# The fourth plain chunk of a gated network: its low weights move from VectorE to GpSimd, and last in its first product

## The chip, the cores and the metric

The kernel runs on one core of a Trainium2 chip. A core has five engines with queues of their own: TensorE (PE: matmuls, and transposes that are matmuls against an identity), VectorE (DVE), ScalarE (ACT), GpSimd (POOL) and SyncE (SP), which here issues the DMA loads and stores. Each runs its instructions in program order and waits at semaphores for the others. The metric is the device time of one execution in microseconds (us); less is better.

## The reference, cut to what matters

The program is one inference step of a trunk of two layers. Each layer mixes tokens by attention and then runs a gated network with a convolution of width 3 between its two projections. 512 latent and 128 context tokens, a width of 1024 and an inner width of 2816 give:

```python
def conv_ffn(h, w_up, conv_w, conv_b, w_down):
    u = h @ w_up
    up = jnp.pad(u, ((0, 0), (1, 1), (0, 0)))
    u = up[:, :-2] * conv_w[0] + up[:, 1:-1] * conv_w[1] + up[:, 2:] * conv_w[2] + conv_b
    a, gt = jnp.split(u, 2, axis=-1)
    return (jax.nn.silu(a) * gt) @ w_down

for l in range(DEPTH):            # DEPTH = 2
    ...                           # attention, norms, residuals
    fp = conv_ffn(hp, ffn_w_up[l], ffn_conv_w[l], ffn_conv_b[l], ffn_w_down[l])
    fs = conv_ffn(hs, ffn_w_up[l], ffn_conv_w[l], ffn_conv_b[l], ffn_w_down[l])
    ...
```

The change is in the first product, `h @ w_up`, of both layers.

## The kernel before, in words

**Tiling.** `h` is kept transposed, features on the partitions, tokens in the columns. The 5632 outputs of `w_up` are worked in 22 pairs of a value chunk and a gate chunk of 128 outputs each; `(p, i)` is pair `p`, value (`i` = 0) or gate (`i` = 1). Products are exact to more than one pass: a weight tile `wr`, loaded from memory by SP (`fetch`, L1195), is cast on ACT to a high part `wh` (L1203), and the rest, `wl = wr - wh`, is made by a subtract (L1204) on DVE or on POOL, whichever `split` is given. In the same way the columns have a high and a low part. `block_product` (L1237) multiplies 512 inputs by 322 columns in twelve matmuls: for each of four blocks of 128 inputs `wh` by the high columns, `wl` by the high columns, and `wh` by the low columns. With `lows=True` the four with `wl` come last.

From the third pair on, a scheme with seven products of half-size blocks in place of eight is used; its weights are sums of weight blocks (`block_sums`, L1224 to L1227), and `value`, `corner` and `sum_parts` split them (tiles `vh`, `vl`, `ah`, `al`, `wh`, `wl`). The first two pairs (`PLAIN = 2`) are four *plain* chunks, `chunks[0]` to `chunks[3]`, each with all eight half-size products, since at that time the columns are not complete: tokens are still coming out of the attention's last projection. `plain0` runs the first two products of a chunk ("11" into a `ux` bank, "21" into a `uy` bank), copies the first on ACT (`c`, L1258) and adds it to the second on DVE (L1329); `plain1` runs the others later.

**What stands around the change.** At that point the last token tile (tile 4) is still being finished (`fin0`): on DVE the residual (L400), a scaling (L412) and a shift (L419), with ACT's sums of squares (L370) and three small POOL instructions between (two `v` at L372, `ro` at L379). Its eight transposes on PE (`tr`, L120) run in two groups of four between the chunks. Behind L419 DVE makes the block differences of the columns (L255, L249, with ACT's casts, L248).

The code names the engine of each step, and a scheduler puts each engine's instructions in an order of its own from the code's order, the dependences and its own estimate of times. So an edit in one line also reorders the queues of DVE, ACT, POOL and SP. `bk.get` and `bk.put` hand out PSUM banks: a product or a group of transposes that takes a bank waits until the bank's last reader is done; the second group of four transposes takes the bank that L1329 of the third chunk reads. The four weight tiles `wr` in `wp` go round as well: a load waits for the cast and the subtract that read the tile before it.

The lines to follow are: L1204 (the subtract), L1329 (the add of a plain chunk), L1348 (which engine subtracts for the fourth chunk), L1355 (the loop that runs the third and fourth chunk) and L1195 (loads).

Of the kernel before, what the change touches and what calls it, by code (L numbers as in the profile page):

```python
# [44 lines left out]
TH = 322  # L45
# [59 lines left out]
def hybrid_step(ctx: ExitStack, tc: tile.TileContext, A, O):  # L105
    nc = tc.nc
# [9 lines left out]
    def mm(*a, **k):  # L116
        pe(nc.tensor.matmul(*a, **k))  # L117
# [10 lines left out]
    def pool(name, bufs=1, side="left", **k):  # L128
        return tc.tile_pool(name=name, bufs=bufs, side=side, reuse_waits="tile", **k)
# [356 lines left out]
    def na_v_put(vt, c, src):  # L486
        return nc.scalar.copy(vt[:, c], src.rearrange("p (a d) -> p a d", a=4))
# [18 lines left out]
    with ExitStack() as s:  # L506
# [155 lines left out]
        for c in range(NT):  # L662
            v_part(7, (c,))
            i = na_v_put(vts_of[0], c, vb[c][:, 0:256])
# [490 lines left out]
    def ffn(l, hT, hT_close, xold, xnew, nxt, todo, late, late_close, side, back, first, fin0, after=None):  # L1155
# [28 lines left out]
        with ExitStack() as s2:  # L1184
# [3 lines left out]
            ws, raws, done = first.ws, first.raws, set(first.ws)  # L1188
            nr = [len(raws)]

            def fetch():
                while nr[0] < len(need) and (nr[0] < 4 or need[nr[0] - 4] in done):
                    p, i = need[nr[0]]
                    raw = wp.tile([P, KC, P], F32, tag="wr", name="wr")
                    nc.sync.dma_start(raw, rows(w_up, 0, 8, (p + i * FC) * P, P))  # L1195
                    raws[p, i] = raw
                    nr[0] += 1

            def pair_of(own, tags, n):
                return [own.tile([P, n, P], F32R, tag=x, name=x) for x in tags]  # L1200

            def split(src, hl, low):
                nc.scalar.copy(hl[0], src)  # L1203
                low.tensor_sub(hl[1], src, f32(hl[0]))  # L1204

            def plain(p, i, low):
                ws[p, i] = pair_of(wp, ("wh", "wl"), KC)
                split(raws[p, i], ws[p, i], low)
                done.add((p, i))
                fetch()  # L1210
# [26 lines left out]
            def block_product(u, w, h, b, first, last=True, lows=False):  # L1237

                seq = [(k, n) for k in range(4) for n in range(3)]
                if lows:  # L1240
                    seq.sort(key=lambda kn: kn[1] == 1)
                for i, (k, n) in enumerate(seq):
                    mm(u, w[n == 1][:, 4 * h + k, :], hT.B[b][n == 2][:, k, :], start=first and i == 0,
                       stop=last and i == 11, skip_group_check=True)
# [11 lines left out]
            def copied(name, p, u):  # L1256
                small[name, p] = sw2.tile([P, TH], F32, tag=name, name=name)
                return nc.scalar.copy(small[name, p], u)  # L1258
# [8 lines left out]
            def block(p, i, j):  # L1267
                c0 = 1 + (2 * TH + 1) * i + TH * j
                return sums(p)[:, c0 : c0 + TH]
# [49 lines left out]
                    q, t = outs.popleft()  # L1319
                    nc.sync.dma_start(actd[q], t)  # L1320

            def plain0(p, i):

                x = banks["p", p, i] = bk.get("ux")
                block_product(x[:, 0:TH], ws[p, i], 0, "11", True)
                c = copied("c1", (p, i), x[:, 0:TH])
                y = bk.get("uy")
                block_product(y[:, 0:TH], ws[p, i], 1, "21", True)
                a = nc.vector.tensor_add(block(p, i, 0), y[:, 0:TH], small.pop(("c1", (p, i))))  # L1329
                bk.put(y)  # L1330
                return c, a
# [13 lines left out]
            chunks = [(p, i) for p in range(PLAIN) for i in range(2)]  # L1345
            plain(*chunks[2], nc.vector)
            fin0.last(*zip(*(plain0(*c) for c in chunks[:2])))
            plain(*chunks[3], nc.vector)  # L1348
            swb = s2.enter_context(pool("swb", 1, side))
            hT.begin(swb, ("22", "1"))  # L1350
            late[0]()
            hT.first(0)
            value(PLAIN, nc.vector)
            for c in chunks[2:]:
                plain0(*c)  # L1355
            late[1]()
            hT.first(1)
            u = banks["x", PLAIN][:, 0:TH]
# [119 lines left out]
    def gqa_w(c0, u, own=None):  # L1478
        return wsplit(rows(wqkv, 2 * u, 2, c0, 512), 2, 512, None, own)

    wkv = []
    hT, hp2, late, xmp = ffn(
        0, hT, hp1.close, lambda t: xres[0][t], lambda t: xres[1][t], (1, 1, 0, NS),
        ((0, 5), (1, 1), (1, 0), (1, 2), (1, 4)), late, xmp.close, "right", "left", first, fin,
# [305 lines left out]
    for hq in range(2):  # L1790
        for n, t in enumerate(((4, 0, 1, 2, 3), (0, 1, 2, 3, 4))[hq]):
# [3 lines left out]
            i = 5 * hq + n  # L1795
# [90 lines left out]
    def y_out(t):  # L1886
        return O["y_sample"][0, t * P : (t + 1) * P, :] if t < 4 else O["y_prompt"][0]

    _, _, _, xmp = ffn(
        1, hT, r_h3.close, lambda t: xres[2][t], y_out, None, ((1, 5),), late, xmp.close, "left", "right", first, fin  # L1890
    )
# [70 lines left out]
```

## Time and profile before

| | us |
|---|---|
| median of 3 runs | 1549.0 (1548.19 to 1549.32) |
| the profiled execution | 1550.43 |
| its span in the profile | 1548.6 |
| PE busy | 1513.5 (98% of the span) |
| DVE busy | 1022.3 (66%) |
| ACT busy | 854.0 (55%) |
| POOL busy | 702.2 (45%) |

The clock that PE was granted was 0.998 of full speed over the span. The stretches that the change touches are at about 360 to 400 us (layer 0) and 1100 to 1140 us (layer 1). In a timeline, a row gives the start, the length, the engine, the line and the tiles (out<-in); `x2` groups neighbouring instructions, and a bracket gives the time that the engine idled ahead of it and what ended the idling. Numbers in matmul shapes are partitions by columns.

### The profile page before, as it was taken

The numbers are of one execution on the slowest core, as the hardware profiler recorded it, in microseconds if no ns is written. First come the engines' busy times: TensorE is split into PE (matmuls) and PEld (weight loads), VectorE is DVE, ScalarE is ACT, GpSimd is POOL, SyncE is SP. The second block draws the span as 40 slices with busy tenths as digits, with TensorE's granted clock in tenths as the row PEclk, the third lists the DMA queues.
The fourth block names the chain that finished last, engine by engine and source line by source line (L and its number), as shares of the span: only waits on it lengthen the run. The fifth ranks groups of instructions, "written<-read, shape, count | busy, mean of one in ns | idle before, by whom it ended". The sixth has DMA issues, their size and how long they took to land.

```text
span 1548.6 us, 26098 instructions
## 1 busy us (share of the span) xinstructions
PE 1513.5 (98%) x9709; PEld 1343.4 (87%) x9709; DVE 1022.3 (66%) x1648; ACT 854.0 (55%) x1624; POOL 702.2 (45%) x606
## 2 busy tenths in 40 slices
PE   6999999999999999999999999999999999999998
PEld 5988998888999999978887878778899999988886
DVE  4553343659877666755757877773988887786554
ACT  5664564646655555554544447763665665564443
POOL 1554564432355455525443464532235666542433
PEclk9999999999999999999999999999999999999999
DMA  9745454253565665388574421015433335447664
GB/s 324 199 123 161 121 134 116 64 189 125 176 225 182 222 190 162 111 279 272 174 238 153 131 67 44 2 34 196 153 115 114 120 110 158 132 161 251 226 220 131
DMA packets 196666, 243.99 MB, mean 158 GB/s; under 512 B 11484, under 2 KB 153020, under 8 KB 196540
## 3 DMA queue, kind: packets, MB, share of 16 engines
q1 hardware_dynamic: 186704, 235.74, 47.8%
q10 hardware_dynamic: 9836, 6.59, 2.5%
q8 instruction: 76, 1.25, 0.3%
q14 instruction: 50, 0.41, 0.1%
HBM read 214.38 MB, written 26.34 MB: 155 GB/s over the span
## 4 chain that ended last, share of the span: by engine, by line
PE 63%; DVE 5%; ACT 2%; issue 2%; POOL 2%; DMA 1%; POOLq 0%; DVEq 0%; ACTq 0%
PE ux L117 18%; PE acc L117 17%; PE uz L117 8%; PE gp L117 5%; PE uy L117 4%; PE po L117 3%; PE y L117 2%; PE s L117 2%; PE tp L120 2%; PE ada L117 1%; DMA wr<-in_ffn_w_down 1%; DVE t L1281 1%; POOL wl L180 1%; DMA wr<-in_ffn_w_up 1%; DVE wl L180 1%
## 5 line engine op out<-in xcount | busy, mean ns | idle before, releaser
L180 POOL TENSOR_TENSOR wl<-wr,wh 128x1024 fp32r<-128x1024 f32 x70 | 173.8, 2487 | 239.8 <-ACT wh L178 228.7
L1204 POOL TENSOR_TENSOR wl<-wr,wh 128x1024 fp32r<-128x1024 f32 x76 | 183.6, 2438 | 46.9 <-ACT wh L1203 43.3
L117 PE MATMUL ux<-B,wh 128*128 128x322 f32 x832 | 200.0, 311 | 0.9 <-ACT u L1258 0.9
L1281 DVE SCALAR_TENSOR_TENSOR t<-C,cw,t 128x644 f32<-128x644 f32 x176 | 156.4, 888 | 51.3 <-ACT t L1279 50.7
L178 ACT CAST wh<-wr 128x1024 fp32r<-128x1024 f32 x140 | 145.5, 1048 | 53.8 <-DMA wr<-in_ffn_w_down 41.1
L117 PE MATMUL acc<-wh,alo 128*128 128x512 f32 x440 | 172.3, 392 | 0.3 <-DVE alo L1173 0.3
L117 PE MATMUL acc<-wl,ahi 128*128 128x512 f32 x440 | 171.9, 391 | 0.5 <-POOL wl L180 0.5
L117 PE MATMUL acc<-wh,ahi 128*128 128x512 f32 x440 | 171.9, 391 | 0.0
L117 PE MATMUL uz<-B,wh 128*128 128x322 f32 x640 | 156.2, 312 | 0.9 <-ACT v L1258 0.9
L117 PEld LDWEIGHTS ux<-B,wh 128*128 128x128 f32 x832 | 143.6, 189 | 3.3 <-issue 1.2
L1173 DVE TENSOR_TENSOR alo<-ain,ahi 128x384 fp32r<-128x384 f32 (+1 forms) x88 | 81.8, 948 | 88.9 <-ACT ahi L1171 88.6
L117 PE MATMUL ux<-B,wl 128*128 128x322 f32 x416 | 129.5, 311 | 3.0 <-DVE wl L1204 3.0
L117 PE MATMUL qk<-hT,wh 128*128 128x384 f32 (+1 forms) x512 | 122.3, 315 | 0.0
L117 PEld LDWEIGHTS uz<-B,wh 128*128 128x128 f32 x640 | 110.9, 189 | 4.4 <-ACT v L1258 1.5
L1204 POOL TENSOR_TENSOR vl<-wr,vh 128x1024 fp32r<-128x1024 f32 x38 | 96.4, 2537 | 24.6 <-ACT vh L1203 24.3
L1203 ACT CAST wh<-wr 128x1024 fp32r<-128x1024 f32 x84 | 84.8, 1049 | 40.9 <-DVE wr L1227 40.6
L1279 ACT ACTIVATE t<-C,cw 128x644 f32<-128x644 f32 x88 | 78.6, 893 | 47.8 <-DVE C L1309 40.2
L180 DVE TENSOR_TENSOR wl<-wr,wh 128x1024 fp32r<-128x1024 f32 x70 | 91.4, 1315 | 19.3 <-ACT wh L178 18.7
L117 PE MATMUL uz<-B,wl 128*128 128x322 f32 x320 | 99.6, 311 | 0.3 <-POOL wl L1204 0.3
L117 PEld LDWEIGHTS acc<-wl,ahi 128*128 128x128 f32 x440 | 82.6, 188 | 18.9 <-POOL wl L180 0.9
L117 PEld LDWEIGHTS acc<-wh,alo 128*128 128x128 f32 x440 | 82.5, 188 | 18.7 <-DVE alo L1173 1.1
L117 PEld LDWEIGHTS acc<-wh,ahi 128*128 128x128 f32 x440 | 82.6, 188 | 17.7
(259 smaller groups left out, 3858.2 us busy)
## 6 DMA issues: line engine op xcount, KB each, us to landing
wr<-in_ffn_w_up SPq DMA_DIRECT2D x88, 512.0 KB
wr<-in_ffn_w_down SPq DMA_DIRECT2D x88, 512.0 KB
wr<-in_ada_w SPq DMA_DIRECT2D x72, 512.0 KB
act<-act SPq DMA_DIRECT2D x44, 321.0 KB
wr<-in_na_w_qkv SPq DMA_DIRECT2D x24, 512.0 KB
mod<-modrow SPq DMA_DIRECT2D x20, 512.0 KB
ain<-act SPq DMA_DIRECT2D x44, 192.0 KB
wf<-in_ada_w SPq DMA_DIRECT2D x16, 512.0 KB
```

The source lines that it names most:

```text
L117: pe(nc.tensor.matmul(*a, **k))
L120: pe(nc.tensor.transpose(*a, **k))
L178: i = nc.scalar.copy(hi, raw)
L180: j = (low or nc.vector).tensor_sub(lo, raw, f32(hi))
L1173: pin(nc.vector.tensor_sub(lo[:, 0 : c1 - c0], ain[:, 0 : c1 - c0], f32(hi[:, 0 : c1 - c0])))
L1203: nc.scalar.copy(hl[0], src)
L1204: low.tensor_sub(hl[1], src, f32(hl[0]))
L1279: nc.scalar.activation(t, taps(0), AF.Identity, bias=cw[:, 3, n : n + 1], scale=cw[:, 1, n : n + 1])
L1281: nc.vector.scalar_tensor_tensor(t, taps(d), cw[:, w, n : n + 1], t, op0=ALU.mult, op1=ALU.add)
```

## The change

The fourth plain chunk's low weights are made by GpSimd, and its first product does its four low-weight matmuls last:

```diff
-            def plain0(p, i):
+            def plain0(p, i, lows=False):
 
                 x = banks["p", p, i] = bk.get("ux")
-                block_product(x[:, 0:TH], ws[p, i], 0, "11", True)
+                block_product(x[:, 0:TH], ws[p, i], 0, "11", True, lows=lows)
...
             plain(*chunks[2], nc.vector)
             fin0.last(*zip(*(plain0(*c) for c in chunks[:2])))
-            plain(*chunks[3], nc.vector)
+            plain(*chunks[3], nc.gpsimd)
...
             for c in chunks[2:]:
-                plain0(*c)
+                plain0(*c, lows=c == chunks[3])
```

Both networks run this code, so each engine's order changes at two places of the program. On POOL, layer 0, around the tile finishing before (`v0` and `ro` are the small instructions, `vl_4780` is a subtract of the fourth gated pair):

```order
L372 TENSOR_SCALAR v0_4369<-sso_4367,v0_4053 128x1
L379 TENSOR_TENSOR ro_4372<-v0_4369,mhalf_74 128x1
L372 TENSOR_SCALAR v0_4488<-sso_4486 128x1
L372 TENSOR_SCALAR v0_4494<-sso_4492,v0_4488 128x1
L379 TENSOR_TENSOR ro_4497<-v0_4494,mhalf_74 128x1
L1204 TENSOR_TENSOR vl_4780<-wr_4420,vh_4779 128x1024
```

and now:

```order
L372 TENSOR_SCALAR v0_4369<-sso_4367,v0_4053 128x1
L379 TENSOR_TENSOR ro_4372<-v0_4369,mhalf_74 128x1
L1204 TENSOR_TENSOR wl_4504<-wr_4409,wh_4503 128x1024
L372 TENSOR_SCALAR v0_4488<-sso_4486 128x1
L372 TENSOR_SCALAR v0_4494<-sso_4492,v0_4488 128x1
L379 TENSOR_TENSOR ro_4497<-v0_4494,mhalf_74 128x1
L1204 TENSOR_TENSOR vl_4780<-wr_4420,vh_4779 128x1024
```

The subtract `wl_4504` of the fourth chunk stands directly behind the `ro` that L400 needs and ahead of the two `v0` and the `ro` that L419 needs.

On DVE, layer 0, from L419 of the last token tile to the L1329 of the fourth chunk (`C_4565<-uy_4552` is the third chunk's, `C_4565<-uy_4583` the fourth's), before:

```order
L419 SCALAR_TENSOR_TENSOR xm_4364<-xm_4364,ro_4497,mod_4360 128x512 x2
L1204 TENSOR_TENSOR wl_4504<-wr_4409,wh_4503 128x1024
L255 TENSOR_TENSOR hF_3968<-hF_3968 128x4x190
L249 TENSOR_TENSOR B221_4513<-hF_3968,B220_4512 128x4x190
L1204 TENSOR_TENSOR vl_4534<-wr_4411,vh_4533 128x1024
L249 TENSOR_TENSOR B11_4515<-hF_3968,B10_4514 128x4x190
L1329 TENSOR_TENSOR C_4565<-uy_4552,c1_4550 128x322
L1204 TENSOR_TENSOR al_4705<-wr_4413,ah_4704 128x512
L1329 TENSOR_TENSOR C_4565<-uy_4583,c1_4581 128x322
```

and now:

```order
L419 SCALAR_TENSOR_TENSOR xm_4364<-xm_4364,ro_4497,mod_4360 128x512 x2
L255 TENSOR_TENSOR hF_3968<-hF_3968 128x4x190
L1204 TENSOR_TENSOR vl_4534<-wr_4411,vh_4533 128x1024
L1204 TENSOR_TENSOR al_4705<-wr_4413,ah_4704 128x512
L249 TENSOR_TENSOR B221_4513<-hF_3968,B220_4512 128x4x190
L249 TENSOR_TENSOR B11_4515<-hF_3968,B10_4514 128x4x190
L1329 TENSOR_TENSOR C_4565<-uy_4552,c1_4550 128x322
L1224 TENSOR_TENSOR wr_4413<-wr_4413 128x512
L1204 TENSOR_TENSOR al_4784<-wr_4507,ah_4783 128x512
L1329 TENSOR_TENSOR C_4565<-uy_4583,c1_4581 128x322
```

The subtract of `wl_4504` is gone; `al_4705`, which stood behind the third chunk's L1329, stands ahead of it; one block sum (L1224) and `al_4784`, which came later, stand ahead of the fourth chunk's.

On SP, the loads and stores with their waits (names in the brackets are semaphores of DVE, ACT, POOL and of DMA queues), before:

```order
L406 DMA xres_0_3_96<-xo_4276 128x1024 [waits DMAHW6_49,DMAHW2_49,DVE_49]
L1195 DMA wr_4413<-in_ffn_w_up 128x8x128 [waits DMAHW3_49,DVE_49]
L1195 DMA wr_4420<-in_ffn_w_up 128x8x128 [waits DVE_49,Activation_49]
L406 DMA xres_0_4_97<-xo_4362 128x1024 [waits DMAHW0_49,DVE_49]
L1195 DMA wr_4507<-in_ffn_w_up 128x8x128 [waits DVE_49,Activation_49]
```

and now:

```order
L406 DMA xres_0_3_96<-xo_4276 128x1024 [waits DMAHW6_49,DMAHW2_49,DVE_49]
L1195 DMA wr_4413<-in_ffn_w_up 128x8x128 [waits DMAHW3_49,DVE_49]
L1195 DMA wr_4420<-in_ffn_w_up 128x8x128 [waits Pool_49]
L1195 DMA wr_4507<-in_ffn_w_up 128x8x128 [waits DVE_49]
L406 DMA xres_0_4_97<-xo_4362 128x1024 [waits DMAHW0_49,DVE_49]
```

The load of `wr_4507` stands ahead of a store of the residual and waits for DVE alone, where the load of `wr_4420` ahead of it waits for POOL's new subtract. On ACT the cast `ah_4783` of `wr_4507` moves from behind the fourth chunk's `c` copy to ahead of the third's.

## Rows read from the trace of the kernel before

**Rows 1.** The page: busy times (part 1), one of PE's costliest groups (part 5).

```profile
PE 1513.5 (98%) x9709; PEld 1343.4 (87%) x9709; DVE 1022.3 (66%) x1648; ACT 854.0 (55%) x1624; POOL 702.2 (45%) x606
...
L117 PE MATMUL ux<-B,wh 128*128 128x322 f32 x832 | 200.0, 311 | 0.9 <-ACT u L1258 0.9
```

**Rows 2.** Timeline of PE, layer 0: start us, length us, what, [idle before <-releaser].

```profile
368.41 0.31 PE L117 MATMUL ux<-B,wl 128*128 128x322 f32 x1
...
373.87 0.42 PE L117 MATMUL ux<-B,wl 128*128 128x322 f32 x1 [1.75 <-DVE wl L1204]
...
377.38 1.27 PE L120 MATMUL tr<-ident,xm 128*128 128x128 f32 x8
```

**Rows 3.** Timeline of PE at the same place of layer 1.

```profile
1114.22 0.41 PE L117 MATMUL ux<-B,wl 128*128 128x322 f32 x1 [1.30 <-DVE wl L1204]
```

**Rows 4.** List of waits of PE's weight loads, 372 to 380 us: total, times, longest.

```profile
PEld tr L120 <- DVE C L1329: 0.2, 1, 0.2
```

**Rows 5.** Timeline of DVE, layer 0, 363 to 384 us.

```profile
363.75 1.42 DVE L419 SCALAR_TENSOR_TENSOR xm<-xm,ro,mod 128x512 f32<-128x512 f32 x2 [1.09 <-POOL ro L379]
...
365.70 1.21 DVE L1204 TENSOR_TENSOR wl<-wr,wh 128x1024 fp32r<-128x1024 f32 x1
...
368.56 1.28 DVE L412 TENSOR_TENSOR xm<-xo,mod 128x512 f32<-128x512 f32 x2
...
371.26 1.42 DVE L419 SCALAR_TENSOR_TENSOR xm<-xm,ro,mod 128x512 f32<-128x512 f32 x2 [1.02 <-POOL ro L379]
372.59 1.22 DVE L1204 TENSOR_TENSOR wl<-wr,wh 128x1024 fp32r<-128x1024 f32 x1
373.73 0.94 DVE L255 TENSOR_TENSOR hF<-hF 128x760 f32<-128x760 f32 x1
374.59 0.94 DVE L249 TENSOR_TENSOR B<-hF,B 128x760 fp32r<-128x760 f32 x1
375.45 1.22 DVE L1204 TENSOR_TENSOR vl<-wr,vh 128x1024 fp32r<-128x1024 f32 x1
376.58 0.94 DVE L249 TENSOR_TENSOR B<-hF,B 128x760 fp32r<-128x760 f32 x1
377.45 0.48 DVE L1329 TENSOR_TENSOR C<-uy,c 128x322 f32<-128x322 f32 x1
377.85 0.68 DVE L1204 TENSOR_TENSOR al<-wr,ah 128x512 fp32r<-128x512 f32 x1
...
381.91 1.50 DVE L262 TENSOR_TENSOR hF<-hF 128x1288 f32<-128x1288 f32 x1
...
383.72 3.42 DVE L263 TENSOR_TENSOR hF<-hF 128x1288 f32<-128x1288 f32 x1
```

**Rows 6.** Timeline of POOL, layer 0.

```profile
364.06 0.86 POOL L379 TENSOR_TENSOR ro<-v,mhalf 128x1 f32<-128x1 f32 x1
...
383.38 2.41 POOL L1204 TENSOR_TENSOR vl<-wr,vh 128x1024 fp32r<-128x1024 f32 x1 [12.15 <-ACT vh L1203]
```

**Rows 7.** Timeline of POOL, layer 1.

```profile
1109.66 0.93 POOL L372 TENSOR_SCALAR v<-sso 128x1 f32<-128x1 f32 x1 [4.04 <-ACT junk L370]
```

**Rows 8.** Timeline of DVE, layer 1.

```profile
1109.25 1.28 DVE L412 TENSOR_TENSOR xm<-xo,mod 128x512 f32<-128x512 f32 x2
...
1111.62 1.42 DVE L419 SCALAR_TENSOR_TENSOR xm<-xm,ro,mod 128x512 f32<-128x512 f32 x2 [0.68 <-POOL ro L379]
...
1117.80 0.48 DVE L1329 TENSOR_TENSOR C<-uy,c 128x322 f32<-128x322 f32 x1
```

**Rows 9.** Timeline of SP, layer 0: the load for the fourth gated pair's gate.

```profile
373.89 0.37 SPq L1195 DMA_DIRECT2D wr<-in_ffn_w_up  x1
```

**Rows 10.** Timeline of ACT, layer 0.

```profile
362.91 1.04 ACT L1203 CAST wh<-wr 128x1024 fp32r<-128x1024 f32 x1
...
374.71 0.83 ACT L248 CAST B<-hF 128x760 fp32r<-128x760 f32 x1 [1.13 <-DVE hF L255]
...
377.66 0.62 ACT L1203 CAST ah<-wr 128x512 fp32r<-128x512 f32 x1 [1.44 <-DMA wr<-in_ffn_w_up]
```

## The prediction

> **What bounds the kernel now.** I read the busy times first. The reader is to see TensorE (PE) busy for 1513.5 of 1548.6 us while VectorE (DVE), ScalarE (ACT) and GpSimd (POOL) stand at 66, 55 and 45% [rows 1]. So an edit on another engine counts only where PE waits for that engine, and its price is the change in such a wait. The second view is PE's order of time around the fourth plain chunk. PE waits there 1.75 us in layer 0 and 1.30 us in layer 1 for the low weights that DVE makes at L1204 [rows 2, 3]: 3.05 us in all, the most that taking these waits away alone can give. The third view is the list of waits just behind. The eight transposes that follow the chunk take 1.27 us, and the list says that their weight load waited 0.2 us for L1329, DVE's add of the third chunk (chunks[2]) [rows 2, 4]. That small wait is the important one: it sits 3.5 us behind the big one, and on DVE the two waits' releasers stand in one unbroken row of work. From the L419 at 371.26 to the L1329 that ends at 377.93 each instruction starts as the one before it ends [rows 5]. If PE comes earlier to the transposes, it waits there for the same row of DVE work. So the question is not how soon the low weights are there, but when DVE reaches L1329 of the third chunk.
>
> The fourth view is that row on DVE, with what starts it, and POOL's beside it. L419 waited for POOL's ro (1.02 us, 371.26) [rows 5]; ro follows two small v on POOL, and these follow the residual work L400 and L412 on DVE. In layer 1 one sees how v is tied to DVE: v, one number per partition, took 0.93 us and ended at 1110.59, just after L412 ended at 1110.53; L419 began 1.09 us after that L412 ended [rows 7, 8].
>
> **The change part by part.**
>
> *Low weights last.* The four low-weight products of the fourth chunk's first product go behind its eight others. The number of matmuls stays. Eight matmuls now run ahead of the first that needs the low weights, so POOL may take until well after the time at which PE waited before. Cost nothing.
>
> *Taken from DVE.* One L1204 of 128x1024, a step of 1.14 us (372.59 to 373.73) [rows 5].
>
> *Added to POOL.* The same subtract; POOL's rows for this shape take 2.41 us [rows 6]. It stands directly behind the ro that ended at 364.92 (364.06 + 0.86), ACT's cast of its high weights had ended by 363.95 (362.91 + 1.04) [rows 10], and so it does not wait until the fourth chunk: it starts about when the L419 beside that ro ends, 365.17 (363.75 + 1.42), and ends at 367.58. PE needs it after 372, so for PE it is early by over 4 us.
>
> *What that does to DVE.* At 365.70 DVE wants to start its own L1204, for the third chunk [rows 5]. The trace shows what becomes of a DVE instruction with two SBUF inputs that starts beside a big POOL subtract: L263 took 3.42 us, where L262, of the same shape, took 1.50. POOL's vl had started at 383.38 and ended at 385.79; L263 ended at 387.14, that is 1.35 us after it [rows 5, 6]. I read this as a full stop: DVE's instruction does nearly all of its 1.50 us after POOL's has ended. Applied to the wl at 365.70 (1.21 us alone, 0.14 of it taken off as in L263's case): it ends at 367.58 + 1.07 = 368.65 instead of 366.91, 1.74 us late. Bounds: 0 if there were no such stop, and 1.9 if nothing is taken off. I take 1.74, since L263's row is the same pair of operations.
>
> [...]
>
> *PE at the third chunk.* Its first low-weight matmul ran at 368.41 [rows 2]; it now waits until about 368.7. That is 0.3 us, and it is lost ahead of the wait below, so it does not add to it.
>
> *The row on DVE behind it.* Everything to L412 is moved by the 1.74 us: L412, 368.56 + 1.28 = 369.84 before, ends at 371.58. From there I use layer 1's 1.09 us for v, v, ro: L419 starts at 372.67, 1.41 late (some slack in layer 0 is used up) [rows 5, 8]. Behind it the new order counts. The fourth chunk's wl (1.14) is gone, but an al, which stood behind L1329 of the third chunk, now stands ahead of it (0.68 long; 0.60 as a step, since each step is 0.08 shorter than the row's length). From L419's start to L1329's end: 1.33 + 0.86 + 1.13 + 0.60 + 0.86 + 0.87 + 0.48 = 6.13 us, where it was 6.67 (371.26 to 377.93) [rows 5]. So L1329 ends at 372.67 + 6.13 = 378.80: **0.87 us later** than before.
>
> *What PE makes of it in layer 0.* With the 1.75 gone and 0.3 added PE reaches the transposes at about 375.9 instead of 377.38, does four of the eight and then waits for L1329 until 378.80. The wait of 1.75 is not gained: it has moved to the transposes and grown to over 2.4, and PE goes on 0.87 later.
>
> *Layer 1.* The same instructions stand there with the same durations. L412 (1109.25 + 1.28 = 1110.53) is followed at once by v, v, ro, so there is no slack: L419 goes from 1111.62 to 1113.36, and L1329 ends at 1113.36 + 6.13 = 1119.49 instead of 1118.28: **1.21 us later** [rows 7, 8].
>
> *A copy on ACT and its load.* The ah cast that ran at 377.66 now stands ahead of the third chunk's c copy, and its load ahead of a store. Issue to cast took 3.8 us (373.89 to 377.66) [rows 9, 10]. The load now goes when DVE's wl of the third chunk is done, at about 368.7; with 3.8 us it is there at 372.5 and costs nothing, since L1329 wants c only at 378.3. With twice that, 376.3, it would still let ah, c and two casts on ACT finish near 379, about 0.5 us per layer. I take 0.
>
> *Later on.* At the start of the gate chunks, in layer 1, a t (L1279) now stands ahead of the u copy on ACT for which PE waited 0.9 us in the whole run [rows 1], and DVE's block sums come earlier by the al that has left them. Bounds -0.6 and +0.9; I take +0.3, nearer to the middle.
>
> **Sum:** 0.87 + 1.21 + 0.3 = +2.4 us. The rows are of an execution of 1550.43 us (span 1548.6), 1.4 above the median 1549.0; a few us in so many do not depend on that, so the forecast is 1549.0 + 2.4 = **1551.4 us**.
>
> **The rivals.**
>
> *A, POOL and DVE do not stop each other (ends not slower).* The wl at 365.70 runs as before, L419 starts at 371.26, and L1329 ends at 371.26 + 6.13 = 377.39, 0.54 earlier; in layer 1 as much (1111.62 + 6.13 = 1117.75). PE gains 1.1 us, 1547.9. For it: L419, the neighbour of ro, took its usual 1.42. Against it: L263's 3.42 and v's 0.93. It decides at one place: whether the third chunk's wl on DVE takes about 1.2 or about 2.9 us. [...]
>
> *B, the whole wait of 3.05 us is gained.* That needs the transposes not to wait for L1329: 1546.0. For it: they waited only 0.2 before. Against it: the DVE row is shorter by 0.54 alone, while PE would come 1.75 earlier. It would need DVE's other work to move too.
>
> *C, the load is what is late.* Two weight loads are now issued within about 1 us (367.6 and 368.7). If they share the DMA engines with more than the load of the row, and the ah cast comes at 377 instead of 372.5, then ah (0.62) and c (about 0.4) are done at 378.1, the two casts for B (0.83 each) [rows 10] at 379.7, L249 at 380.6, and L1329 at 381.0: 2.2 us later than forecast in a layer. In one layer 1553.6, in both 1555.8. Against it: 8 us and more from issue to landing would be twice the row's 3.8.
>
> *D, POOL's subtract starts only behind the residual work,* say as L412 ends at 369.84. Then it runs to 372.25 and stops L419 in place of the wl: L419, 1.42 long, goes on from there, a microsecond later than at 371.26, and L1329 ends at 377.39 + 1.0 = 378.4, 0.46 later than before; in both layers 0.9, 1549.9. Against it: nothing in POOL's order keeps the subtract waiting so long.
>
> **How the numbers follow.** Forecast (+1 to +4) 0.55; A 0.12; B 0.05; C 0.15; D 0.13. About 0.2%, 3.1 us, is what a measurement of this kernel can tell from no change. The forecast's own range is 1550 to 1553.5: about a third of its chance is above +3.1 when the end bounds add up (0.5 from the load in each layer, 0.9 at u). Slower: 0.18 + 0.13 of C = 0.31. Faster: of B most, and a little of A where the order later on helps, 0.07. Within 0.2%: 0.62. The range takes in A, D and one layer of C: 1546.8 to 1554.2.
>
> **What would show it.** Right: POOL's wl near 365.2, DVE's wl of the third chunk taking 2.9 us, L419 over a microsecond late, no wait at the fourth chunk's wl, and a wait of over 2 us at the transposes for L1329, in both layers. Wrong: DVE's wl at 1.2 us (A); a wait of PE at the transposes under 0.5 us (B); an ACT wait for wr ahead of c that ends after 376 (C); POOL's wl that starts after 369 (D).

## The result and the profile after

The changed kernel takes 1553.62 us (median of 7 runs, 1552.59 to 1557.54) against 1549.17 for the kernel before (7 runs, 1547.7 to 1549.7): 4.45 us slower, a ratio of 1.0033 with a 95% interval of 1.0024 to 1.0043. That is a loss clear of the noise. The forecast was +2.4 us, with the chance of "within 0.2%" twice that of "slower"; the time lies 0.1 us above the forecast's own range (1550 to 1553.5) and inside the wider one that takes in the rivals. The forecast's 1549.0 was the median of the first three of these seven runs of the kernel before. The profiled execution of the changed kernel took 1552.95 us, its span is 1551.2.

The busy times say as little as before: PE is at 98%, DVE at 66% as in [rows 1].

```profile
PE 1514.3 (98%) x9709; PEld 1345.8 (87%) x9709; DVE 1028.8 (66%) x1646; ACT 853.3 (55%) x1624; POOL 712.0 (46%) x608
```

The timeline of DVE in layer 0 (columns as in [rows 5]) shows the stop and what it moves:

```profile
361.83 1.42 DVE L419 SCALAR_TENSOR_TENSOR xm<-xm,ro,mod 128x512 f32<-128x512 f32 x2 [1.09 <-POOL ro L379]
...
363.78 2.82 DVE L1204 TENSOR_TENSOR wl<-wr,wh 128x1024 fp32r<-128x1024 f32 x1
...
368.25 1.28 DVE L412 TENSOR_TENSOR xm<-xo,mod 128x512 f32<-128x512 f32 x2
...
370.33 1.41 DVE L419 SCALAR_TENSOR_TENSOR xm<-xm,ro,mod 128x512 f32<-128x512 f32 x2 [0.40 <-POOL ro L379]
...
373.66 0.68 DVE L1204 TENSOR_TENSOR al<-wr,ah 128x512 fp32r<-128x512 f32 x1
...
375.98 0.48 DVE L1329 TENSOR_TENSOR C<-uy,c 128x322 f32<-128x322 f32 x1
```

The third chunk's L1204 takes 2.82 us, where [rows 5] has 1.21. On POOL beside it (columns as in [rows 6]):

```profile
362.97 2.54 POOL L1204 TENSOR_TENSOR wl<-wr,wh 128x1024 fp32r<-128x1024 f32 x1
368.56 0.42 POOL L372 TENSOR_SCALAR v<-sso 128x1 f32<-128x1 f32 x1 [3.04 <-ACT junk L370]
```

The new subtract runs from 362.97 to 365.51; DVE's ends at 366.60, 1.09 us after it. Alone it takes 1.21 us [rows 5], so nearly all of its work was done behind POOL's end, as with L263 (1.35 of 1.50). The two profiles differ by 1.93 us ahead of all this: the same matmul, the first of the third chunk, starts at 368.17 before and at 366.24 after. That comes from the first 80 us of the two executions and is taken off below. PE before, at five places (first product of the third chunk, first of the value weights, in layer 0; the same two and the first of `plain1` in layer 1):

```profile
368.17 0.40 PE L117 MATMUL ux<-B,wh 128*128 128x322 f32 x1
...
378.40 0.39 PE L117 MATMUL ux<-B,vh 128*128 128x322 f32 x1
...
1108.99 0.39 PE L117 MATMUL ux<-B,wh 128*128 128x322 f32 x1
...
1118.76 0.40 PE L117 MATMUL ux<-B,vh 128*128 128x322 f32 x1
...
1122.39 0.31 PE L117 MATMUL ux<-B,wh 128*128 128x322 f32 x1
```

and after, with the wait ahead of the second four transposes:

```profile
366.24 0.39 PE L117 MATMUL ux<-B,wh 128*128 128x322 f32 x1
...
376.52 0.66 PE L120 MATMUL tr<-ident,xm 128*128 128x128 f32 x4 [2.20 <-DVE C L1329]
376.93 0.40 PE L117 MATMUL ux<-B,vh 128*128 128x322 f32 x1
...
1107.91 0.39 PE L117 MATMUL ux<-B,wh 128*128 128x322 f32 x1
...
1118.07 0.66 PE L120 MATMUL tr<-ident,xm 128*128 128x128 f32 x4 [2.22 <-DVE C L1329]
1118.48 0.40 PE L117 MATMUL ux<-B,vh 128*128 128x322 f32 x1
...
1123.65 0.31 PE L117 MATMUL ux<-B,wh 128*128 128x322 f32 x1
```

The wait at the low weights [rows 2, 3] is gone and a wait of 2.2 us stands at the transposes in both layers. Differences after minus before, place by place: -1.93, -1.47 in layer 0; -1.08, -0.28 and +1.26 in layer 1; and +2.37 at the program's last matmul. So PE loses 0.46 us at the transposes of layer 0, 0.80 at those of layer 1, **1.54 between two places of layer 1 where no wait stands at all**, and 0.39 and 1.11 us in the long stretches of gate chunks behind. The sum is 4.30 us, and the medians differ by 4.45.

The 1.54 us are the clock. Busy time by windows of 1 us in layer 1 (stretch, its length, then PE, PEld, DVE, ACT and POOL busy with counts, the granted TensorE clock, DMA share and GB/s):

```profile
1118.00:1119.00 1.00, 0.93 (x7) 0.93 (x8) 1.00 (x3) 0.24 (x1) 0.00 (x0) 1.00 0.00 0
1119.00:1120.00 1.00, 1.00 (x8) 1.00 (x7) 1.00 (x3) 0.97 (x2) 0.00 (x0) 0.76 0.00 0
1120.00:1121.00 1.00, 1.00 (x6) 1.00 (x5) 1.00 (x3) 0.15 (x2) 0.00 (x0) 0.50 0.00 0
1121.00:1122.00 1.00, 1.00 (x5) 1.00 (x5) 1.00 (x3) 0.84 (x2) 0.00 (x0) 0.50 0.00 0
1122.00:1123.00 1.00, 1.00 (x5) 1.00 (x5) 1.00 (x3) 0.00 (x0) 0.00 (x0) 0.53 0.02 8
1123.00:1124.00 1.00, 1.00 (x9) 1.00 (x8) 1.00 (x1) 0.15 (x1) 0.00 (x0) 1.00 0.00 0
```

Behind the wait the granted clock stands at 0.50, the lower of its two levels (1.2 in place of 2.4 GHz), for 0.48 + 1.0 + 1.0 + 0.94 = 3.4 us, and each matmul takes about twice its time. Layer 0 had a wait just as long in this execution and no such stretch.

POOL and DVE met once more behind this place, with the roles changed. In layer 1, timelines of DVE and of POOL:

```profile
1124.41 1.49 DVE L263 TENSOR_TENSOR hF<-hF 128x1288 f32<-128x1288 f32 x1
```

```profile
1124.98 9.19 POOL L1204 TENSOR_TENSOR vl<-wr,vh 128x1024 fp32r<-128x1024 f32 x1 [13.14 <-ACT vh L1203]
```

L263, which took 3.42 us beside POOL's vl in the kernel before [rows 5, 6], started 0.57 us ahead of that subtract here. It took its 1.49 us, and POOL's subtract took 9.19 us in place of 2.41: DVE ran six instructions one behind the other until 1131.87, and POOL's ended 2.3 us after that. In layer 0 POOL's started first (381.90 against 382.86), and L263 took 3.31 us.

### The profile page after: what moved, and what is told of

Its sections match the earlier page's. It is cut to its first block, busy times and chain, and to the rows that moved or that the text cites. A ratio compares the mean times of both kernels' runs of the same rounds, so it can differ in the third digit from the quotient of the medians.

```text
span 1551.2 us, 26092 instructions
## 1 busy us (share of the span) xinstructions
PE 1514.3 (98%) x9709; PEld 1345.8 (87%) x9709; DVE 1028.8 (66%) x1646; ACT 853.3 (55%) x1624; POOL 712.0 (46%) x608
## 5 line engine op out<-in xcount | busy, mean ns | idle before, releaser
L1204 POOL TENSOR_TENSOR wl<-wr,wh 128x1024 fp32r<-128x1024 f32 x78 | 188.7, 2440 | 43.4 <-ACT wh L1203 39.7
L1281 DVE SCALAR_TENSOR_TENSOR t<-C,cw,t 128x644 f32<-128x644 f32 x176 | 156.3, 888 | 50.1 <-ACT t L1279 49.5
L1204 POOL TENSOR_TENSOR vl<-wr,vh 128x1024 fp32r<-128x1024 f32 x38 | 103.7, 2728 | 30.0 <-ACT vh L1203 29.7
```

The lines of the kernel that those rows point to most:

```text
L1281: nc.vector.scalar_tensor_tensor(t, taps(d), cw[:, w, n : n + 1], t, op0=ALU.mult, op1=ALU.add)
```

## The experiments

All ratios are to the kernel before, timed beside each group of experiments on the same chip: 1548.8 us for low_only to low_add_first, 1548.84 for after_again to best1, 1548.58 for after_ah to best2, and 1548.88 for vl_only. The theory: DVE's row of work up to the third chunk's L1329 sets PE, and POOL's subtract stops DVE for its whole length. The rivals: the waits are worth what they show; the loss comes from the reordering (al, ah and its load), not from the stop.

**low_only.** The change without the move to POOL.

```diff
-            plain(*chunks[3], nc.gpsimd)
+            plain(*chunks[3], nc.vector)
```

> Only the order of PE's matmuls changes: the fourth chunk's low-weight products go last in its first product, VectorE keeps the subtract, and the order on all other engines is that of before. Theory (VectorE's row of work up to the third chunk's L1329 sets PE, not the subtract itself): L1329 ends when it did, the wait of 1.75 and 1.30 us at the low weights shrinks by about 1.2 us (eight matmuls of 0.148 instead of one), and the wait at the transposes grows by the same; no gain, 1549.2 within 0.5. Rival (the wait at the low weights is worth what it shows): 1.2 + 1.2 us gained, 1546.8.

Measured: 1549.4 us, ratio 1.0004 (0.9995 to 1.0013). PE in layer 0:

```profile
373.19 0.86 PE L117 MATMUL ux<-B,wl 128*128 128x322 f32 x4 [0.75 <-DVE wl L1204]
...
377.30 0.66 PE L120 MATMUL tr<-ident,xm 128*128 128x128 f32 x4 [1.04 <-DVE C L1329]
```

The wait at the low weights is 0.75 in place of 1.75 us, and the one at the transposes, 0.2 before, is 1.04. One turned into the other; the theory's point, without POOL in it.

**pool_only.** The change without the new order of matmuls.

```diff
-                plain0(*c, lows=c == chunks[3])
+                plain0(*c)
```

> Only the subtract moves to GpSimd; PE keeps the order of before, and all other engines have the order of the changed kernel. Theory: GpSimd's low weights are there over 4 us before PE wants them, so putting them last does nothing: the time of the changed kernel, 1553.6 within 1, with the same wait of about 2.2 us at the transposes. Rival (the new order of PE's matmuls carries part of the loss): clearly below, 1549 to 1551.5.

Measured: 1555.4 us, 1.0045 (1.0032 to 1.0057): no less than the changed kernel, so the order of the products carries none of the loss. It is 1.8 us more than the 1553.6 expected, and outside the 1 us allowed. Layer 0 had the same 2.2 us at the transposes. Layer 1 showed something else, on ACT and on PE:

```profile
1116.93 0.62 ACT L1203 CAST ah<-wr 128x512 fp32r<-128x512 f32 x1 [4.13 <-DMA wr<-in_ffn_w_up]
```

```profile
1120.90 1.11 PE L120 MATMUL tr<-ident,xm 128*128 128x128 f32 x4 [3.87 <-DVE C L1329]
```

The ah cast waited 4.13 us for its load, held the copy and, through the casts of the columns behind it, L249 (which waited 1.61 us for them) and L1329; the wait at the transposes was 3.87 us. It is rival C's mechanism, in one execution. A stretch at the lower clock followed for over 6 us.

**twice.** The orders of before, with POOL's subtract as an extra one.

```diff
-                split(raws[p, i], ws[p, i], low)
+                split(raws[p, i], ws[p, i], pre or low)
+                if pre:
+                    low.tensor_sub(ws[p, i][1], raws[p, i], f32(ws[p, i][0]))
...
-            plain(*chunks[3], nc.vector)
+            plain(*chunks[3], nc.vector, nc.gpsimd)
```

> The orders of the kernel before, with one instruction more per layer: GpSimd makes the fourth chunk's low weights where the changed kernel has it, and VectorE makes them once more where it always did, so PE still waits for VectorE. Theory (VectorE is stopped while GpSimd subtracts): VectorE's subtract for the third chunk takes 2.8 us instead of 1.2, L419 comes about 1.0 us late in layer 0 and 1.4 in layer 1, and with it the low weights and L1329; 2.4 us slower, 1551.6, and up to 1.7 us more per layer if PE's clock falls after its wait, which grows to 2.7 us. Rival (the stop costs nothing, the loss comes from the al and the cast that were moved ahead of L1329): 1549.2 within 0.5.

Measured: 1552.94 us, 1.0025 (1.0016 to 1.0035). On DVE the third chunk's subtract, and on PE the wait at the fourth chunk's low weights, in layer 0:

```profile
364.72 2.82 DVE L1204 TENSOR_TENSOR wl<-wr,wh 128x1024 fp32r<-128x1024 f32 x1
```

```profile
373.88 0.63 PE L117 MATMUL ux<-B,wl 128*128 128x322 f32 x1 [2.47 <-DVE wl L1210]
```

Nothing but an unused result on POOL was added, and the kernel lost 4.1 us: the stop shows by itself, together with what the clock adds, since both layers' waits (2.5 and 2.4 us) were followed by the lower clock. The al and ah stand where they stood before, so the rival (no loss without the reordering) is excluded.

**low_add_first.** low_only, with the third chunk's L1329 ahead of the block differences.

```diff
-            hT.first(0)
+            _, added = plain0(*chunks[2])
+            behind(hT.first(0), added)
             value(PLAIN, nc.vector)
-            for c in chunks[2:]:
-                plain0(*c, lows=c == chunks[3])
+            plain0(*chunks[3], lows=True)
```

> VectorE keeps the subtract, low weights last as in low_only, and the third chunk's L1329 is put ahead of the block differences (L255 and the two L249) on VectorE. Theory: L1329 then comes about 2.6 us earlier, the transposes do not wait, and the shortening of the wait at the low weights becomes a gain: of 1.75 + 0.2 about 0.5 stays in layer 0, of 1.30 + 0.2 about 0.1 in layer 1; 2.8 us faster, 1546.4. Rival (another reader, the casts for the columns or the block sums, is late instead): within 1 us of 1549.2.

Measured: 1549.35 us, 1.0002 (0.9993 to 1.0011). The theory's gain did not come. The transposes no longer wait, but PE waits later, at the u copy:

```profile
374.68 1.03 PE L120 MATMUL tr<-ident,xm 128*128 128x128 f32 x8
...
399.73 0.42 PE L117 MATMUL ux<-B,wh 128*128 128x322 f32 x1 [0.47 <-ACT u L1259]
```

DVE has no idle time between L419 and the conv (L1281, here L1282), so moving one add within that row of work does not make the row end sooner. In this profile PE gained 1.2 us in layer 0 and gave 0.6 back at this wait, where it next needs the end of that row; by the program's last matmul nothing was left of either layer's gain.

**after_again.** The changed kernel once more, without an edit.

> The changed kernel once more, on the chip of the other three, with a second profile. Theory (a wait of PE of over 2 us at the transposes can be followed by a stretch of 3.4 us at half the granted clock, and a load that lands late can lengthen it): the same two waits of 2.2 us or more, the number of such stretches may differ from the one seen, and the times of single executions scatter over more than the 3 us of the kernel before; median 1553 to 1555.

Measured: 1554.0 us (1552.71 to 1557.89), 1.0038 (1.0026 to 1.0051). In this profile the waits were 2.2 and 2.4 us, and both were followed by the lower clock.

**after_corner.** The changed kernel with the al and ah instructions held back.

```diff
-                    corner(PLAIN)
+                    behind(corner(PLAIN)[1], add2)
...
-            corner(PLAIN + 1)
+            hi, lo = corner(PLAIN + 1)
+            behind(hi, copy3)
+            behind(lo, add3)
```

> The changed kernel, but the two al subtracts and the second ah cast are held back behind the adds (L1329) and the copy of the third and fourth chunk, as they stood before. GpSimd's subtract stays where it is, and stops VectorE as in the changed kernel. VectorE then has the third chunk's add behind L419, L255 and vl alone. Theory: L419 is 1.0 late as in the changed kernel, but L1329 ends 2.3 us earlier than there, PE does not wait at the transposes, and the clock does not fall; what PE gains is given back at the u copy as in low_add_first: 1549.2 within 1. Rival (the stop of VectorE costs the time wherever the al stand): 1552 or more.

Measured: 1551.99 us, 1.0021 (1.0012 to 1.0029): the rival's figure, not the theory's. PE in layer 0:

```profile
374.70 1.14 PE L120 MATMUL tr<-ident,xm 128*128 128x128 f32 x8
...
378.63 0.42 PE L117 MATMUL uy<-B,vh 128*128 128x322 f32 x1 [1.01 <-DVE C L1328]
...
401.97 0.41 PE L117 MATMUL ux<-B,wh 128*128 128x322 f32 x1 [1.13 <-ACT u L1257]
```

No wait at the transposes and no slow stretch, as the theory had it; but DVE is as late as in the changed kernel, and PE waits 1.01 us for the fourth chunk's add (here L1328) and 1.13 for u. So the reordering decided where PE waits, and whether the clock falls with it; with the al held back 3.2 us of loss are still there.

**halves.** POOL's subtract in two instructions.

```diff
+                    for c in (slice(0, 4), slice(4, 8)):
+                        low.tensor_sub(lo[:, c, :], raws[p, i][:, c, :], f32(hi[:, c, :]))
```

> The changed kernel, with GpSimd's subtract of the fourth chunk in two instructions of 128x512 in place of one of 128x1024; all orders are those of the changed kernel. Theory (a stop lasts as long as one GpSimd instruction): VectorE's subtract for the third chunk gets its turn after the first half, takes about 1.9 us in place of 2.8, and the row behind it, with the wait at the transposes, is 0.5 to 0.9 us shorter; without the fall of the clock 1550.5 to 1552. Rival (GpSimd's second half goes ahead too, or both share bandwidth): 2.8 us and 1553.6 as before.

Measured: 1556.15 us, 1.0047 (1.0033 to 1.006). POOL and DVE in layer 0:

```profile
362.93 3.67 POOL L1212 TENSOR_TENSOR wl<-wr,wh 128x512 fp32r<-128x512 f32 x2
```

```profile
363.74 1.72 DVE L1204 TENSOR_TENSOR wl<-wr,wh 128x1024 fp32r<-128x1024 f32 x1
...
365.79 2.03 DVE L400 SCALAR_TENSOR_TENSOR xo<-xm,ro,xo 128x512 f32<-128x512 f32 x2
```

The mechanism held: DVE's subtract had its turn between the two halves and took 1.72 us; the second half then stopped L400 (here 2.03, elsewhere 1.40). The time did not follow: the loads that queue behind POOL's last half came later still (the ah cast waited 2.90 and 3.96 us for its load, where the changed kernel's waited 2.18 and 2.43), and PE waited 2.5 and 3.4 us at the transposes.

**best1.** low_add_first, with the vl beside which L263 took 3.42 us [rows 5] subtracted by DVE.

```diff
-            value(PLAIN + 1, nc.gpsimd)
+            value(PLAIN + 1, nc.vector)
```

> low_add_first, and the value weights of the fourth pair (vl) are subtracted by VectorE in place of GpSimd, which stopped L263 (there L264) for 1.9 us in all runs so far. Theory (the gain of low_add_first is given back because VectorE, not PE, sets the stretch up to the u copy): VectorE is 0.8 us earlier at the conv, the wait for u of 0.5 and 0.2 us goes, and 1 to 2 us of the gain stay: 1547.5. Rival (something behind sets the gate chunks, so the gain is given back anyway): 1549 within 0.7.

Measured: 1547.13 us (11 runs), 0.9992 (0.9983 to 1.0001). That line of DVE:

```profile
381.68 1.49 DVE L264 TENSOR_TENSOR hF<-hF 128x1288 f32<-128x1288 f32 x1
```

1.49 us, no wait for u, and 1.7 us less than before, at the edge of what can be told. The "in all runs so far" of the expectation is too wide: L263 was held in the kernel before and in low_add_first, but took 1.49 us in layer 1 of the changed kernel, as shown above, and in both layers of twice.

**after_ah.** The changed kernel with only the second ah cast behind the fourth chunk's copy.

```diff
-            corner(PLAIN + 1)
+            behind(corner(PLAIN + 1), copy3)
```

> The changed kernel with one thing undone: the second ah cast on ScalarE, which waits for a load, stands behind the fourth chunk's copy as in the kernel before, so the copy that the third chunk's L1329 reads no longer queues behind that load. VectorE's order is that of the changed kernel. Theory (where the load lands late, the cast holds the copy and L1329, which lengthens the wait at the transposes from 2.2 to 2.4 to 3.9 us and feeds the slow stretch of the clock; where it lands in time it costs nothing): waits of 2.2 us in both layers, the executions above 1555 go, median 1552 to 1553.5. Rival (the load plays no part): the changed kernel's 1553.6 to 1554 and its scatter.

Measured: 1553.59 us (5 runs, 1552.09 to 1554.91), 1.0034 (1.0021 to 1.0046). The median is the changed kernel's; the waits were 2.2 us in both layers, and no execution was above 1555, where 3 of 12 of the changed kernel were. With 5 executions that points to the load as a part of the scatter, and does not show it.

**fill.** The kernel before, with DVE's subtract moved into DVE's idle time ahead of L419.

```diff
-            fin0.last(*zip(*(plain0(*c) for c in chunks[:2])))
-            plain(*chunks[3], nc.vector)
+            copies, adds = zip(*(plain0(*c) for c in chunks[:2]))
+            fin0.last(copies, adds, plain(*chunks[3], nc.vector))
...
+            behind(low, added[1])
+            behind(self.shifted(NT - 1), low)
```

> The kernel before, with VectorE's own subtract for the fourth chunk put ahead of the last token tile's L419 instead of behind it, into the 1.02 and 0.68 us in which VectorE idles there for GpSimd's ro. No work moves to another engine. Theory (VectorE's row of work decides, and its idle time ahead of L419 is the only free room in it): the wait of 1.75 and 1.30 us at the low weights goes, L419 starts 0.1 and 0.5 us later, L1329 ends 1.0 and 0.6 us earlier, PE waits under 1.1 us at the transposes: 1.7 us faster, 1547.1. Rival (given back at the u copy, as in low_add_first): 1549 within 0.7.

Measured: 1548.88 us, 0.9997 (0.9988 to 1.0006): the theory's 1.7 us did not come. POOL and DVE in layer 0:

```profile
369.74 1.27 POOL L372 TENSOR_SCALAR v<-sso,v 128x1 f32<-128x1 f32 x1 [0.35 <-DVE C L1331]
```

```profile
369.67 1.21 DVE L1205 TENSOR_TENSOR wl<-wr,wh 128x1024 fp32r<-128x1024 f32 x1
371.68 1.42 DVE L419 SCALAR_TENSOR_TENSOR xm<-xm,ro,mod 128x512 f32<-128x512 f32 x2 [0.81 <-POOL ro L379]
```

The second v, which is due in that gap, took 1.27 us and ended with DVE's subtract. The idle time was not free: filled with an instruction of two SBUF inputs it delays the very instruction for which DVE was waiting.

**best2.** best1 with fill's order and after_ah's.

```diff
-            plain(*chunks[3], nc.vector)
+            fin0.last(copies, adds, plain(*chunks[3], nc.vector))
...
-            corner(PLAIN + 1)
+            behind(corner(PLAIN + 1)[0], copy3)
```

> best1 (L1329 of the third chunk ahead of the block differences, the fourth pair's vl by VectorE, low weights last) with the subtract of the fourth chunk put ahead of L419 as in fill, and the second ah cast behind the fourth chunk's copy. Theory: the waits of 0.6 and 0.3 us at the low weights that best1 kept go too, L419 comes 0.1 and 0.5 us later: 0.5 to 1 us faster than best1's 1547.1, 1546.4. Rival (VectorE's row is the bound, so the later L419 takes it back): 1547.1 within 0.5.

Measured: 1547.01 us, 0.9992 (0.9983 to 1.0): no more than best1, the rival's figure. PE waits at no low weights any more, but 0.4 us for the fourth chunk's add.

**vl_only.** The kernel before with best1's one line.

```diff
-            value(PLAIN + 1, nc.gpsimd)
+            value(PLAIN + 1, nc.vector)
```

> The kernel before with one subtract taken from GpSimd and given to VectorE: the value weights (vl) of the fourth pair, beside which L263 took 3.42 us in both layers. Theory (L263 is stopped by that subtract): L263 takes 1.5 us, VectorE is 1.9 us earlier behind it and pays 1.14 us for the vl later, 0.8 us earlier at the conv; PE does not wait there in the kernel before, so 1548.6 within 0.7. Rival (L263 takes 3.4 us for another reason): L263 stays at 3.4 us and VectorE is 1.1 us later at the conv, 1549 to 1550.5.

Measured: 1548.2 us, 0.9996 (0.9987 to 1.0005), no difference that can be told. L263:

```profile
382.51 1.49 DVE L263 TENSOR_TENSOR hF<-hF 128x1288 f32<-128x1288 f32 x1
```

With POOL's subtract taken away from beside it, it takes 1.49 us in place of 3.42. That is the reading on which the prediction's main term rests, now shown by removing the cause.

## Why the prediction was right, and where it was wrong

**Right: the wait moves.** "The wait of 1.75 is not gained: it has moved to the transposes." It did, in both layers, and low_only shows that this needs no POOL: DVE's row up to L1329 is the limit. **Right: the stop.** POOL's subtract started where it was put (362.97, that is 364.90 on the clock of the kernel before), DVE's took 2.82 us where 2.9 was named, and ended 1.09 us after POOL's where 1.07 was worked out. Rival A is excluded by this row, twice and vl_only. Rival B fell with the wait at the transposes, D with POOL's start.

The Trainium skill (SBUF — State Buffer, section Who interferes with whom) states that a VectorE instruction with two SBUF inputs contends with a GpSimd instruction that reads SBUF, and that issue order decides which of the two is blocked. The traces agree in both directions: POOL's subtract held DVE's here (2.82 us), and DVE's row held POOL's vl in layer 1 (9.19 us) and POOL's v in fill (1.27 us).

**Mis-sized: the chain behind L412.** The prediction took layer 1's 1.09 us from L412's end to L419 for both layers. It measured 0.80 (369.53 to 370.33): the first v took 0.42 in place of the 0.93 of [rows 7]. It started 0.31 us behind L412's start in place of 0.41, and ended as the first of L412's two instructions did, where that of [rows 7] ended as the second did. With 0.29 less there, and DVE's subtract ending 0.12 sooner than worked out, the two terms came out at 0.46 and 0.80 us in place of 0.87 and 1.21.

**Missing: the clock.** The step that failed is "PE goes on 0.87 later": it let PE go on at full speed behind a wait of 2.4 us, and the sum had no term for the clock. The cost was 1.54 us in layer 1 of this execution, more than the 1.26 us that the waits of both layers came to. In the trace of before no wait in these stretches was that long, and no such stretch followed. But that trace holds one at the program's start: PE waited 1.54 us until 17.00 and 0.41 until 18.47, and from 18.74 us the clock stood at 0.50 for 3.4 us. So the price was there to be read, though not at these places. The profiles have twelve waits of 2.2 us or more at the low weights or the transposes: two each in the first and the second profile of the changed kernel and in those of pool_only, twice, halves and after_ah. Nine of them were followed by a stretch at the lower clock, which in three began up to 0.9 us before the wait ended; of the waits of 1.8 us or less at these places none was. That such a stretch comes in some executions and not in others fits the changed kernel's scatter (5 us in 7 runs, 2 before): its slowest run, 1557.54 us, has the lowest mean granted clock, 0.994, and its fastest, 1552.59 us, the highest, 0.999.

**Mis-sized: later on.** +0.3 was taken; 0.39 + 1.11 us came. The 0.9 us of [rows 1] from which the bound at u was taken is one wait, at 659.70 us; it does not stand at the start of layer 1's gate chunks, and it is 0.94 us after the change as well. What came instead: PE's rows show waits of 0.27 us for a wl of POOL and 0.46 for L1307 where before had none, and of 0.75 for v where before had 0.19. The first two recur in the profiles of after_again, after_ah, pool_only and halves, where an al stands ahead of the third chunk's L1329 as in the changed kernel, and in none of the others; the last, 0.6 us at 1384 us, also in low_add_first and best2, so it does not need the change. Why they come was not taken apart further, and stays open.

**Rival C** was no rival but a part: the load was late in layer 1 of pool_only and of halves, not in the changed kernel's first profile. That its figure for one layer, 1553.6 us, is the measured median is chance.

In sum, the direction and the mechanism up to the transposes were right. The size was not: the waits came out 0.82 us smaller than the sum had them, the work later on 1.2 us larger, and the stretch at the lower clock, 1.54 us here, was missing. Without it this execution would have lost 2.8 us by the same places, and that this is near the forecast's 2.4 is in part luck, since the two other errors offset each other. The chances, which held "within 0.2%" for the likeliest, had no room for it.

## What to carry to other kernels

Before moving an instruction off a busy engine, ask which row of work ends last for the engine that bounds: here VectorE's row had no idle time that was truly free, so shortening one wait only showed the next. A big GpSimd subtract beside VectorE instructions with two SBUF inputs cost VectorE 1.6 us here where it takes 1.14 us of work away. VectorE instructions with one input in PSUM showed no such price: in the trace of before, the 32 adds of L1300 that began while a GpSimd subtract was running took 0.48 to 0.50 us, as the eight others did. So look for a place where VectorE is idle or reads PSUM before handing work to GpSimd. And price a wait of TensorE of 2 us and more not by its length alone but with the stretch at the lower clock that may follow it.

## What the hardware did that was not expected

The lower clock followed single waits of only 2.2 to 3.9 us in a program in which PE is busy for 98% of the time, for 3.4 us, and for over 6 us in pool_only. A GpSimd instruction with one number per partition (v) was stretched from 0.27 to 1.27 us by one VectorE subtract beside it. And half a microsecond decided which engine was held: the same GpSimd subtract took 2.91 us in layer 0 of the changed kernel, where it started first, and 9.19 us in layer 1, where it started 0.57 us behind a row of VectorE instructions and got no turn between them, while in halves VectorE did get its turn between two GpSimd instructions.
